# Cosine and sine tables of a long convolution loaded as ready high and low parts, sine layers on 128 partitions, one filter split and one gate projection later

## Chip, cores and metric

The program runs on one NeuronCore of a Trainium2 chip. The metric is the device time of one execution in microseconds, the median over several runs. A profile of one execution, taken by the hardware profiler, goes with it. TensorE is called PE below, VectorE DVE, ScalarE ACT, GpSimd POOL and SyncE SP.

## What is computed

One layer of an encoder on 512 tokens of width 1024. Its mixer projects the normalised input once (`w_in`) and feeds two branches. Branch B, which the change touches, is a Hyena convolution. Its filter comes from a small network with two sine layers. The second branch, HGRN2, and the PEER layer that follows (most of the program's time) are the same before and after.

```python
hid = jnp.sin(freq1 * (z @ w1 + b1))            # z: 512 x 33, hid: 512 x 64
hid = jnp.sin(freq2 * (hid @ w2 + b2))
filt = (hid @ w3) * jnp.exp(-t[:, None] * jnp.abs(decay_rate)[None, :])
...
hy = centred_short_conv(hy, conv_w, conv_b)
x0, x1, v = jnp.split(hy, 3, axis=-1)
y_b = x0 * bidirectional_fftconv(v * x1, h_f, h_b, hyena_bias)
y_b = jnp.einsum('blc,cd->bld', y_b, w_branch_b)
g_a, g_b = jnp.split(gates, N_BRANCHES, axis=-1)
merged = jax.nn.sigmoid(g_a) * y_a + jax.nn.sigmoid(g_b) * y_b
```

## The kernel before

Every float32 product is made of three faster products: each operand is split into a high part (a cast by ACT, L93) and a low part (a subtraction by DVE, L94), and `mm3` (L98 to 105) issues high x high (L102), high x low (L103), and low x high or its mirror (L105). A projection of the 512 tokens onto 128 columns is 24 matmuls of 128x512 into a PSUM tile `ps_mm`, of which there are three buffers. Its weights arrive as `wraw` (512 KB, an SP DMA, L129) and become `whi` (ACT) and `wlo` (DVE), two buffers each.

`hyena` treats the 1024 channels in four quarters (`half` = 0 to 3) of 256. A quarter does, for each of its two blocks of 128 channels, three projections with a short convolution (`conv`: ACT scales the PSUM tile into SBUF at L375, DVE adds the neighbours at L376 and L377, and only L377 frees the PSUM tile), the product x1 * v (L542), sums and differences `sd` of mirrored halves (L546 to 550), transposes on PE (L553, L565), and the splits `uo` and `ue`. After them stand the spectrum of the filter (`spectrum(kept, ...)`), the spectrum of the signal multiplied by it (L612 to 614), the next quarter's filter (`filtered`), and the way back (L628 to 651). The transforms are matmuls with tables of cosines and sines (`co`, `so`, `ee`, `ceT`, `soT`, `coT`, `seT`).

- `setup` (L384) loads seven tables of 256 or 258 KB by SP, splits each with a cast on ACT and a subtraction on DVE, loads the alternating row `alt`, and runs the two sine layers on 64 partitions of 512 elements: a matmul (L429, L432), eight DVE steps (L418 to 424), a Sin on ACT (L425).
- `filtered` (L470) loads `fw3` (ACT's queue in the first quarter, L476), casts it (L480), loads the decay twice (`decb`, L486), takes its absolute value (L487) and the windows `win` (L491), multiplies and folds.
- `parted` (L521) splits the folded filter into f1 and f0; in quarters 1 to 3 it stands ahead of the quarter's loop.
- `gates_b` (L260) is a generator: each `next(fill)` is one projection for the branch's gate (columns 72 + db of `w_in`) that gives PE work while DVE is behind. Seven calls stand in the four quarters (one in the middle of quarters 0, 1 and 2, one behind the spectrum of each). Their results go to DRAM (`gbd`) and come back behind the convolution for the sigmoid (L284). The eighth gate is made there and its sigmoid is read straight from PSUM (L267). Then `yh` and `yl` are split from the convolution's result, and the eight projections with `w_b` follow.

The framework's scheduler puts the instructions of each engine in one order; each engine then runs its list strictly in that order, waiting where an input or a buffer is not ready.

Of the kernel before, what the change touches and what calls it, by code (L numbers as in the profile page):

```python
# [215 lines left out]
def mixer(C):  # L216
# [60 lines left out]
    with tc.tile_pool(name="gb", bufs=1) as cp:  # L277
        yh = cp.tile([P, KB, L], F32R, name="yh")
        yl = cp.tile([P, KB, L], F32R, name="yl")
        for db in (KB - 1, *range(KB - 1)):  # L280
            gts[db] = cp.tile([P, L], F32, name=f"gt{db}")
            if db < KB - 1:
                nc.sync.dma_start(gts[db], C.gbd[db])
                nc.scalar.activation(gts[db], gts[db], AF.Sigmoid)  # L284
# [61 lines left out]
def hyena(C, ctx, xh, xl, raws, fill):  # L346
# [37 lines left out]
    def setup():  # L384

        wide = w2.tile([P, 2, 4, HC], F32, name="dftraw", tag="pm", bufs=1).rearrange("p q t c -> p q (t c)")

# [10 lines left out]
        raw = held(7)
        nc.vector.memset(raw[:, : H + 2], 0.0)
        for row in (0, LOW):  # L400
            nc.sync.dma_start(raw[row : row + 1, : H + 2], a["alt"])
        nc.sync.dma_start(raw[:, H + 2 : H + 3], a["altc"])
        nc.scalar.copy(alt, raw[:, : H + 2])
# [2 lines left out]
        layers = cp.tile([P, 2, L], F32, name="layers", tag="f1h")
        scratch = cp.tile([P, 2, L], F32, name="scratch", tag="f1l")
        zT = layers[:33, 0]
        nc.sync.dma_start(zT, a["zT"])
        fw1 = cp.tile([33, FH], F32, name="fw1")  # L410
        nc.sync.dma_start(fw1, a["f_w1"])
        fw2 = cp.tile([FH, FH], F32, name="fw2")
# [14 lines left out]
        hid1 = layers[:FH, 1]  # L427
        ps = C.ps_x.tile([P, L], F32, name="ps_x")
        nc.tensor.matmul(ps[:FH], fw1, zT, start=True, stop=True)  # L429
        sine_layer(hid1, ps[:FH], "f_b1", "f_q1")  # L430
        ps = C.ps_x.tile([P, L], F32, name="ps_x")
        nc.tensor.matmul(ps[:FH], fw2, hid1, start=True, stop=True)  # L432
        hid = layers[:FH, 0]
        sine_layer(hid, ps[:FH], "f_b2", "f_q2")
        nc.scalar.copy(hid2[:FH], hid)
        nc.vector.tensor_sub(hid2[FH:], hid, hid2[:FH])
# [91 lines left out]
    for half in range(D // HC):  # L528
# [974 lines left out]

def constants():
# [3 lines left out]
    def trig(f, k, t):  # L1508
# [38 lines left out]
def layout(inputs):  # L1547
# [67 lines left out]
```

## Time and profile before

| | |
|---|---|
| median of 3 runs (lowest, highest) | 2027.45 us (2026.8, 2028.96) |
| the profiled execution | 2028.04 us, its span 2026.3 us |
| mean granted clock of PE | 0.994 of full speed |
| busy time of DVE, ACT, POOL | 1665.9 us (82%), 993.2 us (49%), 550.3 us (27%) |
| the convolution's part of the span | about 19 to 291 us |

The profile lists busy time by engine, the waits of an engine with what ended them, and the rows of a timeline: start in us, duration in us, engine, line, output and input, and in brackets the idle time ahead of the row with its releaser. Starts of consecutive rows on one engine are nearer together than the durations say, since work is pipelined. A window row gives, for a stretch of time, each engine's busy time, PE's granted clock (PEclk), the busy share of the DMA engines and GB/s.

### The profile page before, as it was taken

The numbers are of one execution on the slowest core, as the hardware profiler recorded it, in microseconds if no ns is written. First come the engines' busy times: TensorE is split into PE (matmuls) and PEld (weight loads), VectorE is DVE, ScalarE is ACT, GpSimd is POOL, SyncE is SP. The second block draws the span as 40 slices with busy tenths as digits, with TensorE's granted clock in tenths as the row PEclk, the third lists the DMA queues.
The fourth block names the chain that finished last, engine by engine and source line by source line (L and its number), as shares of the span: only waits on it lengthen the run. The fifth ranks groups of instructions, "written<-read, shape, count | busy, mean of one in ns | idle before, by whom it ended". The sixth has DMA issues, their size and how long they took to land.

```text
span 2026.3 us, 32320 instructions
## 1 busy us (share of the span) xinstructions
PE 1993.7 (98%) x12417; PEld 1759.9 (87%) x12417; DVE 1665.9 (82%) x2978; ACT 993.2 (49%) x1466; POOL 550.3 (27%) x331
## 2 busy tenths in 40 slices
PE   8979999999999999999999999999999999999998
PEld 6868878888887898889999998888888888888887
DVE  7888863788988647979999968887897889888895
ACT  6545453777775623436767743333333333333333
POOL 0000000000000000000000027777767767666760
PEclk9989999999999999999999999999999999999999
DMA  5212223222212434214767898988988998898884
GB/s 196 99 48 84 73 94 106 84 82 75 73 67 72 146 136 146 99 68 157 227 203 234 276 336 330 333 335 311 362 315 333 339 361 327 337 346 328 327 299 165
DMA packets 161711, 421.99 MB, mean 208 GB/s; under 512 B 13166, under 2 KB 64628, under 8 KB 161430
## 3 DMA queue, kind: packets, MB, share of 16 engines
q1 hardware_dynamic: 118212, 269.09, 37.7%
q0 software_dynamic: 36864, 134.23, 18.0%
q10 hardware_dynamic: 6482, 16.61, 2.3%
q8 instruction: 97, 1.59, 0.3%
q14 instruction: 56, 0.46, 0.1%
HBM read 380.04 MB, written 39.85 MB: 207 GB/s over the span
## 4 chain that ended last, share of the span: by engine, by line
PE 93%; DVE 4%; ACT 1%; issue 1%; DMA 1%; ACTq 0%; DVEq 0%; SPq 0%
PE ps_mm L102 10%; PE ps_mm L105 10%; PE ps_mm L103 10%; PE acc L1195 9%; PE acc L1194 9%; PE acc L1193 9%; PE ps_a L102 9%; PE ps_a L103 8%; PE ps_a L105 8%; PE ps_g L1480 4%; PE ps_x L751 1%; PE ps_s L1325 1%; PE ps_x L102 1%; PE ps_x L105 1%; PE ps_x L103 1%
## 5 line engine op out<-in xcount | busy, mean ns | idle before, releaser
L94 POOL TENSOR_TENSOR ul<-uraw,uh 128x1024 fp32r<-128x1024 f32 x70 | 186.5, 2665 | 588.2 <-DMA gt<-Gd 434.3
L102 PE MATMUL ps_a<-pxh,uh 128*128 128x384 f32 x1024 | 345.8, 338 | 0.3 <-ACT gact L1045 0.3
L103 PE MATMUL ps_a<-pxl,uh 128*128 128x384 f32 x1024 | 342.3, 334 | 0.0
L1195 PE MATMUL acc<-vh,gl 128*128 128x512 f32 x768 | 300.8, 392 | 0.0
L1194 PE MATMUL acc<-vl,gh 128*128 128x512 f32 x768 | 300.0, 391 | 0.0
L1193 PE MATMUL acc<-vh,gh 128*128 128x512 f32 x768 | 299.2, 390 | 0.0
L102 PE MATMUL ps_mm<-xh,whi 128*128 128x512 f32 (+1 forms) x656 | 258.0, 395 | 10.4 <-DVE x L377 10.4
L93 ACT CAST vh<-vraw 128x1024 fp32r<-128x1024 f32 x128 | 134.6, 1052 | 256.9 <-PE acc L1195 127.2
L103 PE MATMUL ps_mm<-xl,whi 128*128 128x512 f32 (+1 forms) x656 | 256.0, 392 | 0.0
L1136 DVE SCALAR_TENSOR_TENSOR grow<-grow,xg 128x1024 f32<-128x1024 f32 x128 | 193.9, 1534 | 50.4 <-DMA grow<-in_u,gidx 50.2
L1148 DVE SCALAR_TENSOR_TENSOR xg<-grow,gw,xg 128x1024 f32<-128x1024 f32 x127 | 195.9, 1542 | 33.7 <-DMA grow<-in_v,gidx 31.9
L1016 POOL IOTA iota<- 128x512 bf16 x1 | 1.2, 1190 | 762.0 <-PE ps_mm L105 762.0
L1107 POOL DMA_INDIRECT grow<-in_u,gidx x128 | 192.5, 1504 | 36.9 <-issue 24.5
L105 PE MATMUL ps_a<-pxh,ul 128*128 128x384 f32 x1024 | 198.4, 334 | 0.0
L103 PEld LDWEIGHTS ps_a<-pxl,uh 128*128 128x128 f32 x1024 | 192.4, 188 | 3.7
L102 PEld LDWEIGHTS ps_a<-pxh,uh 128*128 128x128 f32 x1024 | 192.3, 188 | 3.7 <-ACT gact L1045 0.6
L93 ACT CAST uh<-uraw 128x1024 fp32r<-128x1024 f32 x128 | 134.7, 1052 | 118.3 <-PE ps_a L103 84.5
L94 DVE TENSOR_TENSOR vl<-vraw,vh 128x1024 fp32r<-128x1024 f32 x128 | 186.9, 1461 | 2.5 <-ACT vh L93 2.5
L94 DVE TENSOR_TENSOR wlo<-wraw,whi 128x1024 fp32r<-128x1024 f32 x112 | 136.5, 1219 | 61.4 <-ACT whi L93 29.0
L1107 POOL DMA_INDIRECT grow<-in_v,gidx x128 | 169.9, 1327 | 35.9 <-issue 21.9
L105 PEld LDWEIGHTS ps_a<-pxh,ul 128*128 128x128 f32 x1024 | 179.3, 188 | 0.0
L93 ACT CAST whi<-wraw 128x1024 fp32r<-128x1024 f32 x112 | 117.5, 1049 | 120.1 <-PE ps_mm L103 115.1
(428 smaller groups left out, 3958.0 us busy)
## 6 DMA issues: line engine op xcount, KB each, us to landing
uraw<-in_uT SPq DMA_DIRECT2D x128, 512.0 KB, 6.4
vraw<-in_v SPq DMA_DIRECT2D x128, 512.0 KB, 5.5
wraw<-in_w_in SPq DMA_DIRECT2D x80, 512.0 KB, 3.3
Gd<-Gs SPq DMA_DIRECT2D x12, 2048.0 KB, 9.9
gt<-Gd SPq DMA_DIRECT2D x32, 768.0 KB, 7.4
kept<-gact ACTq DMA_DIRECT2D x22, 384.0 KB, 3.2
gkept<-kept SPq DMA_DIRECT2D x22, 384.0 KB, 6.0
wraw<-in_w_q SPq DMA_DIRECT2D x16, 512.0 KB, 3.2
```

Source lines behind the costliest of these rows:

```text
L93: nc.scalar.copy(hi, src)
L94: return (eng or nc.vector).tensor_sub(lo, src, hi).ins
L102: nc.tensor.matmul(out, ah, bh, start=(i == 0), stop=False)
L103: nc.tensor.matmul(out, *((al, bh) if late else (ah, bl)), start=False, stop=False)
L105: nc.tensor.matmul(out, *((ah, bl) if late else (al, bh)), start=False, stop=(stop and i == n - 1))
L1107: nc.gpsimd.indirect_dma_start(out=t, out_offset=None, in_=tab, in_offset=bass.IndirectOffsetOnAxis(ap=gidx[:, j : j + 1], axis=0))
L1136: nc.vector.scalar_tensor_tensor(t, t, 1.0, xg, op0=ALU.mult, op1=ALU.mult, accum_out=gdot[h][:, i : i + 1])
L1148: nc.vector.scalar_tensor_tensor(gacc, t, gw[h][:, i : i + 1], gacc, op0=ALU.mult, op1=ALU.add)
L1193: nc.tensor.matmul(acc[k][c], gh[:, ts_], vh[:, ds_], start=(r == 0), stop=False)
L1194: nc.tensor.matmul(acc[k][c], gh[:, ts_], vl[:, ds_], start=False, stop=False)
L1195: nc.tensor.matmul(acc[k][c], gl[:, ts_], vh[:, ds_], start=False, stop=(r == NK - 1))
L1480: nc.tensor.matmul(pg[:, q * P : q * P + P], own[:, q], rows[:, q], start=True, stop=True)
```

## The change

Four edits, all in the convolution:

1. The host supplies the tables already split, in two tensors: `tablesco` (128 x 3072 floats, 1.57 MB: co, so, ee) and `tablesceT` (128 x 4128, 2.11 MB: ceT, soT, coT, seT). Each is loaded by one DMA on POOL's queue into a tile of the split type, held back by a one-element ACT copy out of the last of `xh`. The seven casts, seven subtractions and seven SP DMAs go; `alt` becomes one DMA of 128 x 259.
2. The sine layers work on 128 partitions of 256 elements: `fw1` and `fw2` are block-diagonal 128 x 128, `zT` is 128 x 256.
3. `parted` of quarter 1 stands behind the quarter's loop.
4. The `next(fill)` in the middle of quarter 2 goes. Six gates are made in the convolution, and two (db 6 and 7) behind it.

```diff
-        for db in (KB - 1, *range(KB - 1)):
+        for db in (KB - 2, KB - 1, *range(KB - 2)):
             gts[db] = cp.tile([P, L], F32, name=f"gt{db}")
-            if db < KB - 1:
+            if db < KB - 2:
                 nc.sync.dma_start(gts[db], C.gbd[db])
                 nc.scalar.activation(gts[db], gts[db], AF.Sigmoid)
             else:
-                run(fill)
+                next(fill)
...
-            nc.sync.dma_start(raw, a[name])
-            split(nc, hi, lo, raw)
-            dft[name] = (hi, lo)
...
+        zT = layers[:, 0]
+        nc.sync.dma_start(zT, a["zT"])
...
+        for group, w in ((("co", "so", "ee"), H), (("ceT", "soT", "coT", "seT"), H + 2)):
+            t = cp.tile([P, len(group), 2, 2, w], F32R, name="tables" + group[0])
+            nc.scalar.copy(t[:, 0, 0, 0, 0:1], xh[:, KB - 1, L - 1 :])
+            nc.gpsimd.dma_start(t, a["tables" + group[0]])
+            for i, name in enumerate(group):
+                dft[name] = t[:, i, 0], t[:, i, 1]
+        raw = scratch[:, :, :].rearrange("p a b -> p (a b)")
+        nc.sync.dma_start(raw[:, : H + 3], a["alt"])
         nc.scalar.copy(alt, raw[:, : H + 2])
         nc.scalar.copy(altc, raw[:, H + 2 : H + 3])
...
-        if half:
+        if half > 1:
             fe, fo = parted(*folded)
...
+        if half == 1:
+            fe, fo = parted(*folded)
...
-        if half < D // HC - 1:
+        if half < 2:
             next(fill)
```

ACT near the start, right behind the casts of `xh` (`fw` is the raw of `fw3`, `whi` the high part of the next projection's weights, `x_333` and `vv` the short convolutions of the first block). Before:

```order
L476 DMA fw_612<-in_f_w 64x2x256 x2
L93 CAST soh<-dftraw 128x512
L93 CAST eeh<-dftraw 128x512
L486 DMA decb<-in_f_decay 128x256
L93 CAST whi<-wraw 128x1024
L375 ACTIVATE x_333<-ps_mm,vec 128x512
L480 CAST fw3h<-fw_612 128x512
L93 CAST coTh<-dftraw 128x512
L93 CAST whi<-wraw 128x1024
L375 ACTIVATE vv<-ps_mm,vec 128x512
```

and after:

```order
L469 DMA fw_577<-in_f_w 64x2x256
L479 DMA decb<-in_f_decay 128x256 x2
L473 CAST fw3h<-fw_577 128x512
L93 CAST whi<-wraw 128x1024
L375 ACTIVATE x_333<-ps_mm,vec 128x512
L402 CAST alt<-scratch 128x258
L403 CAST altc<-scratch 128x1
L480 ACTIVATE decb<-decb 128x512
L93 CAST whi<-wraw 128x1024
L484 ACTIVATE win<-decb,vec 128x512
L375 ACTIVATE vv<-ps_mm,vec 128x512
```

The cast of `fw3` now stands ahead of the third projection's `whi`, and `alt`, `decb` and a window stand ahead of the fourth's `whi` and of `vv`. On PE the first block's transposes stand behind 19 matmuls of the third projection, before behind 28 (all 24 of it and 4 of the fourth).

DVE in quarter 1 ahead of the point where a PSUM tile comes free for PE (L377 of `x_1014` before, of `x_979` after: the tile x0 of quarter 1 in both; `x_1115` is x1 of its second block, `vv` that block's v). Before:

```order
L516 TENSOR_TENSOR pm<-once 128x2x256
L94 TENSOR_TENSOR f1l<-pm,f1h 128x1024
L368 TENSOR_TENSOR um<-ps_x,um 1x128
L94 TENSOR_TENSOR f0l<-pm,f0h 128x1024
L376 SCALAR_TENSOR_TENSOR x_1014<-ps_mm,vec,x_1014 128x511
L376 SCALAR_TENSOR_TENSOR vv<-ps_mm,vec,vv 128x511
L377 SCALAR_TENSOR_TENSOR x_1014<-ps_mm,vec,x_1014 128x511
```

and after:

```order
L509 TENSOR_TENSOR pm<-once 128x2x256
L368 TENSOR_TENSOR um<-ps_x,um 1x128
L376 SCALAR_TENSOR_TENSOR x_979<-ps_mm,vec,x_979 128x511
L376 SCALAR_TENSOR_TENSOR x_1115<-ps_mm,vec,x_1115 128x511
L377 SCALAR_TENSOR_TENSOR x_979<-ps_mm,vec,x_979 128x511
L377 SCALAR_TENSOR_TENSOR x_1115<-ps_mm,vec,x_1115 128x511
L376 SCALAR_TENSOR_TENSOR vv<-ps_mm,vec,vv 128x511
L94 TENSOR_TENSOR wlo<-wraw,whi 128x1024
L377 SCALAR_TENSOR_TENSOR vv<-ps_mm,vec,vv 128x511
L94 TENSOR_TENSOR f1l<-pm,f1h 128x1024
```

The splits f1l and f0l have moved behind the release. On PE, 17 projection matmuls stood between the transposes ahead of that wait and the wait; now there are 4, and 48 instead of 24 stand between the wait and quarter 1's filter spectrum. Eleven fewer stand ahead of quarter 0's filter spectrum.

ACT behind the convolution (`gt` the gates, `yh` the high part of the convolution's result, `whi` that of `w_b`). Before:

```order
L93 CAST yh<-yb 128x512 x5
L284 ACT_TABLE_LOAD
L284 ACTIVATE gt_2787<-gt_2787 128x512
L267 ACTIVATE gt_2760<-ps_mm 128x512
L284 ACTIVATE gt_2790<-gt_2790 128x512
L284 ACTIVATE gt_2793<-gt_2793 128x512
L284 ACTIVATE gt_2796<-gt_2796 128x512
L284 ACTIVATE gt_2799<-gt_2799 128x512
L284 ACTIVATE gt_2802<-gt_2802 128x512
L284 ACTIVATE gt_2805<-gt_2805 128x512
L93 CAST yh<-yb 128x512 x3
L93 CAST whi<-wraw 128x1024 x9
```

and after:

```order
L93 CAST yh<-yb 128x512 x5
L284 ACT_TABLE_LOAD
L284 ACTIVATE gt_2751<-gt_2751 128x512
L267 ACTIVATE gt_2691<-ps_mm 128x512
L284 ACTIVATE gt_2754<-gt_2754 128x512
L284 ACTIVATE gt_2757<-gt_2757 128x512
L284 ACTIVATE gt_2760<-gt_2760 128x512
L284 ACTIVATE gt_2763<-gt_2763 128x512
L284 ACTIVATE gt_2766<-gt_2766 128x512
L93 CAST yh<-yb 128x512 x3
L267 ACTIVATE gt_2724<-ps_mm 128x512
L93 CAST whi<-wraw 128x1024 x10
```

One sigmoid of a gate from DRAM has gone, one of a gate in PSUM has come, behind `yh`. The first `w_b` weights, cast during the convolution before, are now the first of the ten `whi` behind that sigmoid.

More of the change, by code (lines that the diff above doesn't have):

```diff
@@ L398, in setup @@
[L398 to L402, printed above, removed]
+        layers = cp.tile([P, 2, H], F32, name="layers", tag="f1h")
+        scratch = cp.tile([P, 2, H], F32, name="scratch", tag="f1l")
+        zT = layers[:, 0]
+        nc.sync.dma_start(zT, a["zT"])
+        fw1 = cp.tile([P, P], F32, name="fw1")
+        nc.sync.dma_start(fw1, a["f_w1"])
@@ new lines, in setup @@
+        fw2 = cp.tile([P, P], F32, name="fw2")
+        nc.sync.dma_start(fw2, a["f_w2"])
+        for group, w in ((("co", "so", "ee"), H), (("ceT", "soT", "coT", "seT"), H + 2)):
[5 more added lines that the diff above has]
+        raw = scratch[:, :, :].rearrange("p a b -> p (a b)")
@@ L403, in setup @@
+        nc.sync.dma_start(raw[:, : H + 3], a["alt"])
         nc.scalar.copy(alt, raw[:, : H + 2])
         nc.scalar.copy(altc, raw[:, H + 2 : H + 3])
[L406 to L412, printed above, removed]
@@ L425, in sine_layer @@
             nc.scalar.activation(dst, arg, AF.Sin)
[L427 to L436, printed above, removed]
+        hid1 = layers[:, 1]
+        ps = psum()
+        nc.tensor.matmul(ps, fw1, zT, start=True, stop=True)
+        sine_layer(hid1, ps, "f_b1", "f_q1")
+        ps = psum()
+        nc.tensor.matmul(ps, fw2, hid1, start=True, stop=True)
+        hid = layers[:, 0]
+        sine_layer(hid, ps, "f_b2", "f_q2")
+        for i in range(2):
+            own, other = slice(i * FH, i * FH + FH), slice((1 - i) * FH, (1 - i) * FH + FH)
+            ns = slice(i * H, i * H + H)
+            nc.scalar.copy(hid2[own, ns], hid[own])
+            nc.vector.tensor_sub(hid2[other, ns], hid[own], hid2[own, ns])
     def odd(dst, mat, fb, src):
@@ L1501, in top16, with short @@
     nc.vector.max_index(idx[:, 8:16], val[:, 8:16], rest)
+def short(t):
+    b = np.ascontiguousarray(t, np.float32).view(np.uint32)
+    return ((b + np.uint32(0x7FF) + ((b >> np.uint32(12)) & np.uint32(1))) & np.uint32(0xFFFFF000)).view(np.float32)
 def constants():
@@ L1525, in constants @@
          "soT": blk(np.concatenate([trig(np.sin, 2 * n + 1, n).T, sign, zero], 1)),
-         "alt": np.concatenate([sign[:, 0], [1.0, 0.0]])[None].astype(np.float32),
-         "altc": sign[:P].astype(np.float32), "ident": np.eye(P, dtype=np.float32)}
+         "ident": np.eye(P, dtype=np.float32)}
+    for group, w in ((("co", "so", "ee"), H), (("ceT", "soT", "coT", "seT"), H + 2)):
+        out = np.zeros((P, len(group), 2, 2, w), np.float32)
+        for i, name in enumerate(group):
+            t = c.pop(name)
+            hi = short(t)
+            out[:, i, 0, :, : t.shape[2]] = hi
+            out[:, i, 1, :, : t.shape[2]] = short(t - hi)
+        c["tables" + group[0]] = out
+    c["alt"] = np.zeros((P, H + 3), np.float32)
+    c["alt"][[0, 32], : H + 2] = np.concatenate([sign[:, 0], [1.0, 0.0]])
+    c["alt"][:, H + 2 :] = sign[:P]
     s = np.arange(P)[:, None] % HALF
@@ L1540, in constants @@
     order = rows(q, H, back, H + P, np.arange(L - 1, H + P, -1), P, np.arange(H + 1, H + P))
-    c["zT"] = np.ascontiguousarray(z[order].T)
+    c["zT"] = np.zeros((P, H), np.float32)
+    for i in range(2):
+        c["zT"][i * (P // 2) : i * (P // 2) + z.shape[1]] = z[order[i * H : i * H + H]].T
     c["pair"] = np.array([PAIR_ID], np.float32)
@@ L1567, in layout @@
     out["v"] = ca(A["peer_v"][0])
-    out["f_w1"] = ca(A["filt_w1"][0])
-    out["f_w2"] = ca(A["filt_w2"][0])
+    for name, w in (("f_w1", A["filt_w1"][0]), ("f_w2", A["filt_w2"][0])):
+        out[name] = np.zeros((P, P), np.float32)
+        for o in (0, P // 2):
+            out[name][o : o + w.shape[0], o : o + w.shape[1]] = w
     out["f_w3"] = ca(A["filt_w3"][0])
@@ L1579, in put @@
         if v.shape[0] == 64:
-            vec[:64, o] = v
+            vec[:64, o] = vec[64:, o] = v
         else:
```

16 lines of the change are left out of this document (4 added, 12 removed).

## Prediction

> **What bounds the kernel now.** I read the page's busy times first, then PE's list of waits (in all, times, longest, in us).
>
> ```profile
> PE 1993.7 (98%) x12417; PEld 1759.9 (87%) x12417; DVE 1665.9 (82%) x2978; ACT 993.2 (49%) x1466; POOL 550.3 (27%) x331
> ```
>
> ```profile
> PE ps_mm L102 <- DVE x L377: 10.4, 1, 10.4
> ...
> PE ps_mm L102 <- ACT yh L93: 3.3, 1, 3.3
> PE ps_x L804 <- ACT vh L715: 1.7, 1, 1.7
> ```
>
> PE is busy for 98% of the span, so a transfer, a cast or a subtraction taken off another engine is worth nothing unless PE waited for it. The convolution holds two waits that are worth anything: 10.4 us in quarter 1, behind DVE's convolution step that frees a PSUM tile, and 3.3 us behind the convolution, for `yh`. Each costs more than its length, as the windows of one microsecond show (the last three numbers are PEclk, the DMA share and GB/s).
>
> ```profile
> 122.00:123.00 1.00, 0.00 (x0) 0.00 (x0) 1.00 (x3) 0.88 (x4) 0.00 (x0) 0.77 0.00 0
> ...
> 136.00:137.00 1.00, 1.00 (x5) 0.77 (x5) 0.94 (x3) 0.74 (x3) 0.00 (x0) 0.91 0.93 336
> ...
> 289.00:290.00 1.00, 0.00 (x0) 0.00 (x0) 0.00 (x0) 1.00 (x3) 0.00 (x0) 0.89 0.00 0
> ...
> 636.00:637.00 1.00, 0.47 (x4) 0.47 (x5) 1.00 (x3) 0.68 (x2) 0.00 (x0) 1.00 0.32 102
> ```
>
> ```profile
> 130.63 0.77 PE L102 MATMUL ps_mm<-xh,whi 128*128 128x512 f32 x1 [10.38 <-DVE x L377]
> ...
> 139.37 0.28 PE L102 MATMUL ps_x<-f1h,coh 128*128 128x256 f32 x1
> ```
>
> The clock granted is 1.00 or 0.50, so a mean of 0.77 means that it fell 2.3 us into the long wait (which began at 130.63 - 10.38 = 120.25), and 0.91 that it rose at 136.18. From 130.63 to there PE ran at half speed: 5.55 us for 2.8 us of work, so 2.8 us lost. At 289 it fell likewise, 2.0 us into the 3.3-us wait (whose end, 291.04, is quoted below). Behind the 1.7-us wait at L804 it stayed at 1.00. A wait of up to 1.7 us therefore costs itself, one of 3.3 us costs itself and 2.8 us, and between them I can't tell.
>
> **The sine layers** save on PE's path. The rows below are the two layers' matmuls.
>
> ```profile
> 53.66 1.07 PE L429 MATMUL ps_x<-layers,fw 33*64 33x512 f32 x2
> ...
> 65.76 1.07 PE L432 MATMUL ps_x<-layers,fw 64*64 64x512 f32 x2
> ```
>
> They take some 1.0 us each. Half the columns make that 0.5 each, so -1.0 us. The shorter DVE and ACT steps and the table casts and subtractions save only what PE waits for, below.
>
> **The start.** The views: PE, the chain of waits (its DMA row), ACT with its DMA issue, and DVE.
>
> ```profile
> 29.27 0.40 PE L102 MATMUL ps_mm<-xh,whi 128*128 128x512 f32 x1
> ...
> 36.67 0.33 PE L553 MATMUL ps_x<-ident,sd 128*128 128x128 f32 x1 [0.86 <-DVE sd L546]
> ```
>
> ```profile
> 22.21 6.64 DMA fw<-in_f_w
> ```
>
> ```profile
> 26.56 1.04 ACT L93 CAST whi<-wraw 128x1024 fp32r<-128x1024 f32 x1
> ...
> 28.93 0.62 ACT L480 CAST fw3h<-fw 128x512 fp32r<-128x512 f32 x1 [0.64 <-DMA fw<-in_f_w]
> ...
> 31.02 0.77 ACT L375 ACTIVATE vv<-ps_mm,vec 128x512 f32<-128x512 f32 x1
> 31.35 0.34 ACTq L486 DMA_DIRECT2D decb<-in_f_decay  x1
> ...
> 32.73 0.41 ACT L403 CAST alt<-dftraw 128x258 fp32r<-128x258 f32 x1
> ...
> 35.13 0.63 ACT L487 ACTIVATE decb<-decb 128x512 f32<-128x512 f32 x1 [0.94 <-DMA decb<-in_f_decay]
> 35.79 0.72 ACT L491 ACTIVATE win<-decb,vec 128x512 f32<-128x512 f32 x1
> ```
>
> ```profile
> 35.12 0.69 DVE L542 TENSOR_TENSOR x<-vv,x 128x512 f32<-128x512 f32 x1
> 35.72 0.69 DVE L481 TENSOR_TENSOR fw3l<-fw,fw3h 128x512 fp32r<-128x512 f32 x1
> 36.32 0.29 DVE L546 TENSOR_TENSOR sd<-x 128x129 f32<-128x129 f32 x1
> ```
>
> ```profile
> 25.00:30.00 5.00, 5.00 (x41) 4.87 (x41) 3.40 (x5) 3.32 (x5) 0.00 (x0) 1.00 0.93 306
> ```
>
> Here the change adds a wait. `whi` of the third projection now queues on ACT behind `fw3h`, and `alt`, `decb` and a `win` queue ahead of the next `whi` and of `vv`, whose product feeds the transposes PE stands before. These small loads share the DMA engines, 93% busy at 306 GB/s already, with 3.7 MB of tables. No row shows a plain DMA on POOL's queue or a DMA that fills a split type, so I bound the landing times. `fw` still lands at 28.85 if the tables only take the place of the seven table loads that ran beside it; earlier if they start late. `decb` is now issued at about 23.7 (an estimate from 22.21: two short copies and two more issues of 0.3 to 0.6); it took 3.8 us in the rows (31.35 to 35.1), and `fw` 6.6 us in the busiest stretch, which gives 27.5 to 30.3. The worst is that it lands last: 3.7 MB of tables and 1.4 MB of other loads at 306 GB/s from 22.2 on is 38.9.
>
> I take `fw` at 28.85 and `decb` no later than 31.6. Then fw3h ends at 29.5, `whi` takes 1.04 and PE starts the third projection at 30.6, not 29.27: 1.3 us. ACT goes on with x (ends 31.2), alt and altc (31.6), decb (32.2), whi (33.2), win (33.8) and vv (34.6). DVE adds two convolution steps (0.66 each), the product (0.60 from 35.12 to 35.72) and sd (0.29): 36.75. PE reaches the transposes 19 matmuls in, at 30.6 + 19 x 0.228 = 34.9, and waits 1.85 us. Both waits are near 1.7, so full clock. Against the 0.86 us of before: **+2.3 us**. From 31.6 on every microsecond of `decb` counts, and the clock falls besides: `decb` at 38.9 gives +12.5. If both land in time (`fw` by 26, `decb` by 28.6), vv ends at 31.6, sd at 33.8 against PE's 33.6: -0.6.
>
> **The wait in quarter 1.** Between quarter 0's product and the release DVE is without a gap but one of 0.59 us.
>
> ```profile
> 98.85 0.69 DVE L612 TENSOR_TENSOR t<-ps_x,kA 128x512 f32<-128x512 f32 x1 [0.92 <-PE ps_x L105]
> ...
> 119.50 0.42 DVE L368 TENSOR_TENSOR fm<-pm,fm 1x256 fp32r<-1x256 f32 x1 [0.59 <-ACT fm L367]
> ...
> 125.77 1.21 DVE L94 TENSOR_TENSOR f1l<-pm,f1h 128x1024 fp32r<-128x1024 f32 x1
> 126.99 0.28 DVE L368 TENSOR_TENSOR um<-ps_x,um 1x128 fp32r<-1x128 f32 x1
> ...
> 128.43 0.74 DVE L376 SCALAR_TENSOR_TENSOR x<-ps_mm,vec,x 128x511 f32<-128x511 f32 x1
> 129.09 0.74 DVE L376 SCALAR_TENSOR_TENSOR vv<-ps_mm,vec,vv 128x511 f32<-128x511 f32 x1
> 129.75 0.74 DVE L377 SCALAR_TENSOR_TENSOR x<-ps_mm,vec,x 128x511 f32<-128x511 f32 x1
> ```
>
> PE starts that stretch of DVE's (0.92 us of waiting at 98.85), and in the new order it does so 11 matmuls (2.5 us) and the sine layers' 1.0 us earlier: 3.5 us. What stood at 125.77 stands at 122.27. Then um 0.28, two steps of 0.66 and one of 0.74 free the tile at 124.6 instead of 130.5, and PE goes on at 124.75. But of the 17 matmuls that ran ahead of the wait only 4 are left. PE stops at 120.25 - 3.5 - 13 x 0.228 = 113.8 and waits 10.95 us, no less than now. Behind it stand 48 matmuls, not 24: 10.9 us, 2.8 for the clock, 0.5 for transposes (139.37 - 130.63 less 24 matmuls and the 2.8), so quarter 1's filter spectrum starts at 138.95 instead of 139.37. From the start to here that is **-0.4 us** in all, the sine's -1.0 within it. So the split's new place brings the release forward and the order gives it back. If DVE gained none of the 3.5 us it would be +3.1; if the 24 were done ahead of the wait after all, -5.9.
>
> **Quarter 2 and behind the convolution.** A gate is 24 matmuls, 5.48 us (279.87 to 285.35, below). Taking it out of quarter 2 makes PE come 5.5 us sooner to products of DVE; the next row shows the cover.
>
> ```profile
> 208.56 0.69 DVE L612 TENSOR_TENSOR t<-ps_x,kA 128x512 f32<-128x512 f32 x1 [4.94 <-PE ps_x L105]
> ```
>
> DVE sat 4.9 us idle there waiting for PE; without the gate it is just ready, and I charge 0 (0.6 at worst). Quarter 3 has no such gate now, and no wait of it is on PE's list. The gate comes back behind the convolution, where PE's rows and ACT's are:
>
> ```profile
> 279.87 0.40 PE L102 MATMUL ps_mm<-xh,whi 128*128 128x512 f32 x1
> ...
> 285.35 0.39 PE L102 MATMUL ps_mm<-yh,whi 128*128 128x512 f32 x1
> ...
> 291.04 0.80 PE L102 MATMUL ps_mm<-yh,whi 128*128 128x512 f32 x1 [3.26 <-ACT yh L93]
> ```
>
> ```profile
> 282.23 2.71 ACT L93 CAST yh<-yb 128x512 fp32r<-128x512 f32 x5 [0.76 <-DVE yb L651]
> ...
> 287.26 3.21 ACT L284 ACTIVATE gt<-gt 128x512 f32<-128x512 f32 x6
> 290.38 1.65 ACT L93 CAST yh<-yb 128x512 fp32r<-128x512 f32 x3
> ```
>
> Before, this place loses 3.3 + 2.8 = 6.1 us. After, on the same clock of times, the second gate ends at 290.83. ACT has five sigmoids instead of six at 0.52 (ends 289.86), `yh` (1.65, 291.5), the sigmoid of the second gate (0.5, 292.0), and only then `w_b`'s first `whi` (1.04, 293.05), for which PE waits until 293.2: 2.4 us. `yh` is no longer late; that cast is. At half clock afterwards the place loses 5.2: **-0.9 us**; with the clock kept, -3.7. I take the half clock, since both falls came within 2.3 us. [...]
>
> **Sum:** 2.3 - 0.4 - 0.9 = +1.0 on the profiled execution's 2028.04, so **2029.0 us**. That execution was 0.6 above the median of 2027.45; a measurement of this kernel can tell about 0.2%, 4.1 us, from no change.
>
> **Rivals.**
> 1. *The tables hold up the small loads* (slower). It decides once `decb` lands behind 31.6. For it: 3.7 MB against 306 GB/s is 12 us of all engines. Against: round robin could let small loads through. If the DMA engines work the tables off in blocks, a block of eight rows of 12 KB (98 KB at 306/16 GB/s each) holds an engine 5.1 us and one of eight of 16.5 KB 6.9 us, and `decb` comes between the two or behind, at about 36: vv ends at 39.0, sd at 41.2, PE waits 6.3 + 1.3 - 0.86 and loses 2.8 of clock: +9.6 in place of 2.3, so 2036.3. [...]
> 2. *The clock stays up behind the convolution*: 2.8 less, 2026.2. For it: 2.4 us is nearer to 1.7 than to 3.3.
> 3. *The small loads land early and the clock stays up* (faster): -0.6 - 0.4 - 3.7, 2023.3. For it: POOL's queue may start late. Against it: `fw` was late in the rows without the tables' extra bytes.
> 4. *The wait in quarter 1 does shrink*: -5.9 in place of -0.4, 2023.5. Against it stands the order.
>
> **Chances:** forecast 0.28, rival 1 0.28, rival 2 0.17, rival 3 0.17, rival 4 0.10. Rival 1 is slower unless `decb` lands before 33; 3 and 4 lie at the edge of 0.2%. So faster 0.20, same 0.51, slower 0.29. The range leaves out the far ends of 1, 3 and 4: 2022.0 to 2037.0.
>
> **What would show it.** Right: a wait for `sd` of about 2 us at 35 us; a wait of about 11 us for L377 near 114 to 125; one of about 2.4 us for `whi` behind the convolution; none in quarters 2 and 3. Wrong: ACT idle for `decb` or `alt` past 32 us with PE's clock at 0.50 near 40 (rival 1); a wait in quarter 1 under 8 us (rival 4); PE waiting for `tablesco` or `tablesceT`.

## The result, and the profile after

The changed kernel takes 2037.53 us in the median of 5 runs (2036.17 to 2041.99), against 2027.51 before on the same chip: a ratio of 1.0053, 95% interval 1.0038 to 1.0068, so slower. The prediction of 2029.0 us (2022.0 to 2037.0) was wrong. Rival 1, that the tables hold up the small loads, had given 2036.3. The profiled execution took 2040.89 us with a span of 2038.7, 12.4 us more than the span before.

PE's list of waits after the change (in all, times, longest, in us):

```profile
PE ps_x L546 <- DVE sd L539: 13.4, 4, 12.5
PE ps_mm L102 <- DVE x L377: 11.1, 1, 11.1
...
PE ps_mm L102 <- ACT whi L93: 2.4, 1, 2.4
```

The waits in quarter 1 (11.1 us) and behind the convolution (2.4 us for `whi` instead of 3.3 for `yh`) are those forecast. The one for `sd` was 0.9 us at its longest before, was forecast at 1.85, and is 12.5. ACT's timeline around it shows whom everybody waits for:

```profile
22.23 1.09 ACTq L479 DMA_DIRECT2D decb<-in_f_decay  x2
26.30 0.62 ACT L473 CAST fw3h<-fw 128x512 fp32r<-128x512 f32 x1 [4.41 <-DMA fw<-in_f_w]
26.82 1.05 ACT L93 CAST whi<-wraw 128x1024 fp32r<-128x1024 f32 x1
27.78 0.77 ACT L375 ACTIVATE x<-ps_mm,vec 128x512 f32<-128x512 f32 x1
39.87 0.41 ACT L402 CAST alt<-scratch 128x258 fp32r<-128x258 f32 x1 [11.33 <-DMA scratch<-in_alt]
...
40.28 0.62 ACT L480 ACTIVATE decb<-decb 128x512 f32<-128x512 f32 x1
40.81 1.03 ACT L93 CAST whi<-wraw 128x1024 fp32r<-128x1024 f32 x1
...
42.37 0.76 ACT L375 ACTIVATE vv<-ps_mm,vec 128x512 f32<-128x512 f32 x1
```

`fw` is early (26.30), so the third projection loses nothing. Then ACT stands 11.33 us before the cast of `alt`, and the fourth projection's `whi` and the scaling of `vv` stand behind it in ACT's list. `alt` was issued on SP right behind a weight load, with the tables issued on POOL at the same time (first two fences: the issues on SP and on POOL; third: the list of DMAs from 18 to 60 us with their size and the median time from issue to landing):

```profile
22.34 0.61 SPq L129 DMA_DIRECT2D wraw<-in_w_in  x1
22.99 0.43 SPq L401 DMA_DIRECT2D scratch<-in_alt  x1
```

```profile
22.11 0.72 POOL L397 DMA_DIRECT2D tablesco<-in_tablesco  x1 [21.65 <-ACT tablesceT L396]
22.82 0.58 POOL L397 DMA_DIRECT2D tablesceT<-in_tablesceT  x1
```

```profile
q0 software_dynamic: 288, 3.69, 23.0%
...
tablesceT<-in_tablesceT POOLq DMA_DIRECT2D x1, 2064.0 KB, 16.8
tablesco<-in_tablesco POOLq DMA_DIRECT2D x1, 1536.0 KB, 10.7
...
decb<-in_f_decay ACTq DMA_DIRECT2D x2, 128.0 KB, 11.0
```

The tables land at 22.82 + 16.8 = 39.6, and `alt`, of 130 KB, with them. POOL's queue (q0) moved its 3.69 MB in 288 packets, one for each row of 12 or 16 KB and a few more.

On PE the loss is the wait and a stretch at half clock behind it (PEclk is 0.50 from 45 to 50 us and 0.85 from 50 to 51); the rows are the end of the wait, the first sine matmul, and the filter spectra of quarters 1 and 2 (before: 53.66, 139.37, and 202.14 in the next fence):

```profile
45.81 0.48 PE L546 MATMUL ps_x<-ident,sd 128*128 128x128 f32 x1 [12.54 <-DVE sd L539]
...
67.11 0.59 PE L419 MATMUL ps_x<-layers,fw 128*128 128x256 f32 x2
...
151.86 0.28 PE L102 MATMUL ps_x<-f1h,tablesco 128*128 128x256 f32 x1
...
209.72 0.28 PE L102 MATMUL ps_x<-f1h,tablesco 128*128 128x256 f32 x1
...
301.01 0.50 PE L102 MATMUL ps_mm<-yh,whi 128*128 128x512 f32 x1 [2.41 <-ACT whi L93]
...
394.78 1.50 PE L799 MATMUL ps_x<-vh,KT 128*128 128x128 f32 x12
```

```profile
202.14 0.28 PE L102 MATMUL ps_x<-f1h,coh 128*128 128x256 f32 x1
...
385.29 1.50 PE L804 MATMUL ps_x<-vh,KT 128*128 128x128 f32 x12
```

The execution after began its transposes of the input 0.43 us earlier (10.48 against 10.91). From there on, against before:

| stretch | measured | forecast |
|---|---|---|
| to the first sine matmul | +13.9 | +2.3 |
| to quarter 1's filter spectrum (84.75 against 85.71) | -1.0 | -0.4 |
| to quarter 2's (57.86 against 62.77), less a gate of 5.48 | +0.6 | 0 |
| to the first `vh,KT` matmul of HGRN2 (185.06 against 183.15), the gate back | -3.6 | -0.9 |

With the early beginning that is +9.5, nearly the +10.0 of the medians. The profiled execution lost another 2.7 us between 1080 and 1680, in the PEER layer, whose lists of instructions are the same before and after (its row of 1.1 us for `vl`, L1189, is part of it).

### The profile page after: what moved, and what is told of

The parts are those of the page before. It is cut to its first block, busy times and chain, and to the rows that moved or that the text cites. A ratio compares the mean times of both kernels' runs of the same rounds, so it can differ in the third digit from the quotient of the medians.

```text
span 2038.7 us, 32292 instructions
## 1 busy us (share of the span) xinstructions
PE 1992.7 (98%) x12417; PEld 1759.5 (86%) x12417; DVE 1660.7 (81%) x2971; ACT 985.8 (48%) x1461; POOL 550.3 (27%) x333
## 4 chain that ended last, share of the span: by engine, by line
PE 80%; DVE 2%; issue 2%; DMA 1%; ACT 0%; POOL 0%; DVEq 0%; POOLq 0%; ACTq 0%
PE ps_a L102 8%; PE ps_a L103 8%; PE ps_a L105 8%; PE ps_mm L102 8%; PE ps_mm L103 8%; PE ps_mm L105 8%; PE acc L1189 8%; PE acc L1190 8%; PE acc L1188 8%; PE ps_g L1475 4%; PE ps_x L746 1%; PE ps_s L1320 1%; DVE grow L1131 1%; DMA grow<-in_u,gidx 1%; DMA gkept<-kept 1%
## 5 line engine op out<-in xcount | busy, mean ns | idle before, releaser
L1189 PE MATMUL acc<-vl,gh 128*128 128x512 f32 x768 | 300.5, 391 | 1.1 <-DVE vl L94 1.1
L102 PE MATMUL ps_mm<-xh,whi 128*128 128x512 f32 (+1 forms) x656 | 258.1, 395 | 11.1 <-DVE x L377 11.1
L1143 DVE SCALAR_TENSOR_TENSOR xg<-grow,gw,xg 128x1024 f32<-128x1024 f32 x127 | 191.3, 1507 | 25.2 <-DMA grow<-in_v,gidx 23.4
```

What stands on the lines that cost most here:

```text
L102: nc.tensor.matmul(out, ah, bh, start=(i == 0), stop=False)
L1143: nc.vector.scalar_tensor_tensor(gacc, t, gw[h][:, i : i + 1], gacc, op0=ALU.mult, op1=ALU.add)
L1189: nc.tensor.matmul(acc[k][c], gh[:, ts_], vl[:, ds_], start=False, stop=False)
```

## The experiments

In all of them the time is compared with the kernel before on the same chip. A short name stands for each kernel.

### The tables back (tables_back)

```diff
-            nc.gpsimd.dma_start(t, a["tables" + group[0]])
+            nc.sync.dma_start(raw, a[name])
+            split(nc, hi, lo, raw)
```

> The changed kernel with its first edit undone: the seven tables are loaded raw by SP and split by ACT and DVE as before; the sine layers on 128 partitions, the later split in quarter 1, the missing gate in quarter 2 and the one-piece load of `alt` stay. Theory (the tables' DMA holds up `alt`): the two traces put the loss before the first sine matmul, 13.9 us there (53.66 - 10.91 = 42.75 us from the first transpose before, 67.11 - 10.48 = 56.63 after), and a gain behind it: -1.0 up to quarter 1's filter spectrum, +0.6 in quarter 2, -3.6 behind the convolution. So this kernel should take 2027.5 - 4.0 = 2023.5 us, with no wait for `sd` over 1.5 us. Rival A (the loss comes from one of the other edits, the order of ACT's list among them): it stays near 2037. Rival B (the four edits only gain together): about 2027.5.

2026.07 us, ratio 0.9992 (0.9983 to 1.0001). The wait for `sd` is 1.7 us at its longest:

```profile
PE ps_mm L102 <- DVE x L377: 11.2, 1, 11.2
...
PE ps_x L552 <- DVE sd L545: 2.2, 2, 1.7
```

So the loss is the first edit's, and rival A is out. The other three together gain 4.1 us in this trace up to HGRN2, as expected, but 1.9 in the median, and the interval reaches no change.

### Shorter rows: 1, 4 and 8 KB (small_rows, rows4k, rows8k)

```diff
-            t = cp.tile([P, len(group), 2, 2, w], F32R, name="tables" + group[0])
+            t = cp.tile([P, len(group), 2, 2, w + 2], F32R, name="tables" + group[0])[:, :, :, :, :w]
```

That is small_rows; rows4k leaves the two spare floats once a table, rows8k once for two tables (three DMAs, the `ceT` group first).

> The changed kernel with one difference: each table row of 256 or 258 floats gets two more floats of room in the SBUF tile, so that the same 3.7 MB on the same queue at the same time go in pieces of 1 KB instead of 12 and 16 KB. The order of every engine is that of the changed kernel. Theory with shared bandwidth (the tables were issued first and take the DMA engines' time, whatever their pieces): `alt` lands with the tables again, near 40, and the time stays at 2037 (2034 to 2040). Theory with long pieces (the DMA engines take a piece from each queue in turn, and `alt` stands behind the pieces of four other SP loads, each of which lets a table row of 12 or 16 KB by): with 1 KB pieces `alt` lands by 30 and the wait for `sd` falls below 3 us: 2024 to 2028.

> The changed kernel with the tables' rows in pieces of 4 KB (one piece a table), between the 1 KB of small_rows and the 12 and 16 KB of the changed kernel; all else stays. Theory (DMA engines take pieces from the queues in turn, so that a queue's share goes with the length of its pieces): `alt` lands between small_rows' 31.3 and the changed kernel's 39.9, near 35, the time lies between 2029.75 and 2037.4, near 2033. Rival (one threshold: short enough pieces all act alike): as small_rows, 2029 to 2030. Rival B (only the number of bytes counts, and small_rows was better because POOL's queue fills more slowly with 3616 pieces): near 2037.

> The changed kernel with its table rows in pieces of 8 KB: `ceT` with `soT` and `coT` with `seT` as one piece each (8.25 KB), `co` with `so` as one of 8 KB, `ee` one of 4 KB, the `ceT` group first, one DMA more on POOL's queue; all else stays. It stands between 4 KB (`alt` lands at 31.7, hardly later than the 30.3 without any table in flight) and 12 to 16 KB (39.9). Theory (each DMA engine takes pieces from its queues in turn; about 16 pieces of SP's queue, its share of the weights and of `alt`, stand ahead when the tables start, so that 16 table pieces go by): 16 x 8.25 KB at the 22 GB/s of one engine are 6 us: `alt` lands at 35 to 37, the time is 2033 to 2035. Rival (up to some length pieces act alike): 31 to 32.5 and 2029 to 2030.5. Rival B (above 4 KB the queue is held until the tables are through): near 39, 2036 or more.

Measured: small_rows 2029.75 us (1.0007; 0.9998 to 1.0016), rows4k 2029.73 (1.0010; 1.0001 to 1.0020), not the 2033 that was expected of it, and rows8k 2032.94 (1.0023; 1.0013 to 1.0032). ACT's cast of `alt`, which starts as soon as `alt` has landed, in small_rows, rows4k and rows8k:

```profile
31.32 0.41 ACT L402 CAST alt<-scratch 128x258 fp32r<-128x258 f32 x1 [3.39 <-DMA scratch<-in_alt]
```

```profile
31.75 0.41 ACT L403 CAST alt<-scratch 128x258 fp32r<-128x258 f32 x1 [3.96 <-DMA scratch<-in_alt]
```

```profile
35.11 0.41 ACT L404 CAST alt<-scratch 128x258 fp32r<-128x258 f32 x1 [6.64 <-DMA scratch<-in_alt]
```

To compare executions that did not begin at the same moment, count from SP's first issue of this stretch, that of `zT` (L389): 20.68, 20.52 and 20.13 in these three, 20.89 in the changed kernel and 20.76 in tables_late (below), where no table is in flight and `alt` is cast at 30.32. The same bytes, issued on the same queue at the same point, then delay `alt` by 1.1 us in pieces of 1 KB, 1.7 at 4 KB, 5.4 at 8 KB and 9.4 at 12 and 16 KB. An estimate of the turns: SP's queue has 16 pieces an engine in the weights and `alt` if they are spread evenly (two times 128 rows over 16 engines), and 16 pieces of the tables at 22 GB/s an engine (353 GB/s of the changed kernel's window from 25 to 30 us, over 16 engines) are 0.7, 3.0, 6.0 and 10.4 us. So the theory of turns, each of which lets a piece of the tables by, came out for rows8k, which was told ahead; for rows4k it had asked for more than was found, and the time there was the rival's. That pieces of up to 8 KB act alike is out, and so is a pure share by bytes (rival B); that pieces of up to 4 KB act nearly alike is not.

The trace's records of the single pieces show the turns themselves. From 27 to 36 us in the changed kernel POOL's queue began 203 pieces, SP's 198 and ACT's 203 (those of 4 bytes left out). The pieces of `alt` begin in rounds there, the first ones at 31.56, 32.27, 32.97 and 33.68, and in alt_pool (below) in rounds of 16, 0.71 us apart; a piece of 16.5 KB at 22 GB/s is 0.75 us. Shorter pieces went by more than one at a turn: from 27 to 30 us 192 on POOL's queue against 139 and 112 at 4 KB, 688 against 145 and 135 at 1 KB. One thing beside the length differs: the tables' first piece begins 3.1 us after the issue of `zT` in the changed kernel, but 5.4, 5.5 and 5.8 us after it at 8, 4 and 1 KB. So part of the step from 8 KB to 12 and 16 KB is the earlier beginning; why it is earlier stays open.

### The tables later (after_small, tables_late)

```diff
-            nc.scalar.copy(t[:, 0, 0, 0, 0:1], xh[:, KB - 1, L - 1 :])
+            nc.gpsimd.tensor_copy(t[:, 0, 0, 0, 0:1], x0[:, n, 0:1])
```

(tables_late, with n = 0 for `tablesco` and 1 for `tablesceT`; after_small copies from `alt` and from `decb`.)

> The changed kernel with the tables held back until the small loads have landed: POOL copies one element out of `alt` (after its cast) and out of `decb` ahead of each table's DMA; everything else stays. Theory (the tables hold up `alt` and `decb`): both land by 28, ACT casts `alt` right behind the short convolution at 28.6 instead of 39.87, the wait for `sd` is below 2 us, and the 13.9 us of the start go: 2023.5, up to 3 more if the tables, now at 29 to 41, hold up the weights of the sixth projection (2023 to 2027). Rival A (`alt` is late because it stands behind the weights on SP's queue): it lands near 40 as before: 2037. Rival B (the order of ACT's and PE's lists costs the time, with `alt` on time): a wait of 6 us or more for `sd` remains: 2030 or more.

> The changed kernel with the tables held back further: POOL copies the first element of `tablesco` out of the first block's x0 and that of `tablesceT` out of the second block's, so that the two loads start near 47 and 60 us, apart from each other. Theory: no load of the start is disturbed, and each table load (5 and 7 us of all DMA engines) fits beside the weights' loads: 2023.5 (2022.5 to 2025), about the same as with the tables behind the small loads or up to 3 us better. If the weights' loads are what the tables disturb, a wait for `whi` appears near 50 to 70 us and the time is 2026 or more. Rival A (the start's loss is not the tables' DMA): 2037.

2028.52 us (1.0003; 0.9994 to 1.0012) and 2028.37 (1.0001; 0.9992 to 1.0010): 9 us of the changed kernel's 10 come back, but not the 13.9 that both were to bring. What is left is at the same place. PE's waits and ACT's list in tables_late, and its first transposes and first sine matmul on PE:

```profile
PE ps_x L546 <- DVE sd L539: 4.3, 3, 3.5
```

```profile
30.32 0.41 ACT L402 CAST alt<-scratch 128x258 fp32r<-128x258 f32 x1 [3.34 <-DMA scratch<-in_alt]
...
32.02 1.04 ACT L93 CAST whi<-wraw 128x1024 fp32r<-128x1024 f32 x1
32.96 0.77 ACT L375 ACTIVATE vv<-ps_mm,vec 128x512 f32<-128x512 f32 x1
```

```profile
10.44 1.11 PE L206 MATMUL ps_x<-ident,xn 128*128 128x128 f32 x4 [0.28 <-DVE xn L249]
...
57.23 0.59 PE L419 MATMUL ps_x<-layers,fw 128*128 128x256 f32 x2
```

With no table in flight `alt` still lands 7.4 us after its issue, behind a weight load of 512 KB on the same queue, and 1.7 us of short steps follow. PE waits 3.5 us and then runs at half clock for a while (PEclk is 0.50 from 38 to 39 us and 0.60 from 39 to 40). So rivals A and B of after_small each had a part of it.

### `alt` away from ACT, and the order on ACT (alt_pool, order_only, small_late)

```diff
-        nc.scalar.copy(alt, raw[:, : H + 2])
+        nc.gpsimd.tensor_copy(alt, raw[:, : H + 2])
...
```

```diff
+        with tc.issue_after(C.first_block):
+            nc.scalar.copy(alt, raw[:, : H + 2])
...
+            with tc.issue_after(C.first_block):
+                nc.scalar.activation(decb, decb, AF.Abs)
```

The first is alt_pool (`altc` goes to POOL too). The second is order_only (on the changed kernel) and small_late (on tables_late): `C.first_block` is ACT's step L375 for the first block's `vv`, and the casts of `altc` and `fw3` move behind it as well.

> The changed kernel with one difference: the casts of `alt` and `altc` are made by POOL, which is idle there, instead of ACT; the tables are loaded as in the changed kernel. So ACT no longer waits for `alt`, but still for `decb`. Theory (the tables hold up both, `alt` to 39.8 and `decb` to about 33.9, from its issue at 22.8 and the 11.0 us of its landing): the absolute value of `decb` starts near 34 instead of 40.28, PE waits 6 to 7 us for `sd` instead of 12.5, and the time is about 2031. Rival A (`decb` too lands with the tables, near 39): 2036 or more. Rival B (`decb` had landed by 28, only `alt` was late): a wait under 3 us, 2027 or less.

> The changed kernel with its tables loaded at the start as they are, and only ACT's list changed: the casts of `alt`, `altc` and `fw3` and the absolute value of `decb` stand behind the first block's `vv`. Theory (the tables' load costs only through what stands behind it on ACT's list): ACT waits for `alt` until 39.8 all the same, but the third and fourth projections' weights and `vv` are out by then; what then is late is the fifth projection's `whi` (needed near 38.7, out near 44 behind alt, `fw3h`, decb and two windows): a wait of 3 to 5 us with some half clock: 2027 to 2031. Rival A (nothing else is late): 2023.3, as small_late. Rival B (the weights' loads on SP suffer too, so that PE waits for the fourth projection's `whi` already): 2033 or more.

> The kernel with the tables held back until the blocks' x0 (tables_late), and in it the casts of `alt`, `altc` and `fw3` and the absolute value of `decb` stand on ACT behind the first block's `vv` instead of ahead of it. tables_late still lost 4.0 us before the first sine matmul, with no table in flight: ACT waited 3.3 us for `alt`, and four short steps stood ahead of the `whi` and `vv` that the transposes need. Theory (that order is the rest of the start's loss): `vv` is scaled by 30 and PE waits under 1 us for `sd`; first sine matmul within 0.6 us of before's; 3.5 to 4 us less than tables_late's 2028.37, so 2024.5. Rival (the rest lies in the place of the transposes on PE, 8 matmuls earlier than before, or in the weights' loads): a wait of 2 us or more remains, 2027 or more.

alt_pool: 2037.33 us (1.0047; 1.0033 to 1.0060), no better. Taking `alt` off ACT's list uncovers `decb`, which lands with the tables as well (rival A; my 33.9 was wrong):

```profile
38.72 0.63 ACT L480 ACTIVATE decb<-decb 128x512 f32<-128x512 f32 x1 [10.45 <-DMA decb<-in_f_decay]
```

order_only: 2033.44 us (1.0031; 1.0021 to 1.0042). The time is rival B's, the cause another: `whi` and `vv` are out by 28.9, but the cast of `fw3` now stands behind `alt` on ACT, and on DVE the low part of `fw3` (`fw3l`, L475) stands ahead of the last step of `vv`, the product and `sd`. So DVE waits 8.4 us for ACT and PE 8.3 for `sd`. I had expected 3 to 5, behind the fifth `whi`, and overlooked DVE's list. ACT, DVE and PE:

```profile
28.13 0.78 ACT L375 ACTIVATE vv<-ps_mm,vec 128x512 f32<-128x512 f32 x1
37.45 0.41 ACT L403 CAST alt<-scratch 128x258 fp32r<-128x258 f32 x1 [8.54 <-DMA scratch<-in_alt]
...
37.86 0.61 ACT L474 CAST fw3h<-fw 128x512 fp32r<-128x512 f32 x1
```

```profile
38.51 0.69 DVE L475 TENSOR_TENSOR fw3l<-fw,fw3h 128x512 fp32r<-128x512 f32 x1 [8.37 <-ACT fw3h L474]
```

```profile
40.97 0.47 PE L550 MATMUL ps_x<-ident,sd 128*128 128x128 f32 x1 [8.32 <-DVE sd L543]
```

small_late: 2023.26 us (0.9977; 0.9968 to 0.9986), the first kernel faster than before. No wait for `sd` of more than 0.7 us is left, and the first sine matmul comes 0.7 us sooner after the first transposes than before. So the start's 13.9 us have two parts: 9.8 are the tables loaded so early (the changed kernel against tables_late, 56.6 and 46.8 us from the first transpose to the first sine matmul), 8.0 of them their long rows (48.6 us in small_rows); and the rest, with 0.7 that before had lost too, is the list of ACT. The two rows of small_late, 42.1 us apart:

```profile
10.48 1.12 PE L206 MATMUL ps_x<-ident,xn 128*128 128x128 f32 x4 [0.27 <-DVE xn L249]
...
52.56 0.59 PE L420 MATMUL ps_x<-layers,fw 128*128 128x256 f32 x2
```

### The other edits one by one (sine_only, tb_split, tb_gate)

sine_only is the kernel before with the second edit alone. tb_split and tb_gate are tables_back with the third or the fourth edit undone:

```diff
-        if half > 1:
+        if half:
             fe, fo = parted(*folded)
...
```

```diff
-        if half < 2:
+        if half < D // HC - 1:
             next(fill)
...
```

> The kernel before with the second edit alone: the sine layers on 128 partitions; tables, `parted` and gates as before. The prediction's term: -1.0 us. Theory now: PE's list moves with it (in the kernel with old tables and the early split quarter 0's filter spectrum came 3.4 us earlier from the first sine matmul on), but PE then stands before the same DVE stretch in quarter 1, and its wait grows from 10.4 to about 13 us: -1.0 to +0.5, not to be told from no change (2027 to 2028.5), and the trace shows quarter 1's filter spectrum no more than 1 us earlier than before. Rival (the move is worth its 3.4 us): 2025 or less.

> The kernel with the tables loaded the old way (tables_back) and in it the third edit undone as well: `parted` of quarter 1 stands ahead of the quarter's loop again. Theory (the later split brings the release forward and the order on PE gives it back): from the first sine matmul to quarter 1's filter spectrum tables_back took 1.27 us less than before, 1.0 of it the sine layers'; so undoing the split costs about 0.3 us, 2026.4 against 2026.07. Rival (the wait for L377 shrinks by the later split): 2 us or more are lost, 2028 or more, and the wait is longer than tables_back's 11.2 us. Rival 2 (the later split itself costs, since only 4 matmuls run ahead of the wait): 2 to 3 us are gained, 2024 or less.

> The kernel with the tables loaded the old way (tables_back) and in it the fourth edit undone as well: seven gates in the convolution again, one behind it. Theory: in tables_back's trace the edit takes 4.6 us off quarter 2 and gives 1.9 back behind the convolution, where a 2.4-us wait for `whi` keeps PE's clock at 1.00 instead of the 3.3-us wait for `yh` with 2.8 us of half clock: 2.7 us in that execution. In executions where the clock falls in the 2.4-us wait too, the edit is worth about nothing. So undone it should cost 1 to 2.7 us: 2027 to 2028.8, with the 3.3-us wait back. Rival (the edit is worth nothing or costs, as the wait for `whi` replaces the one for `yh`): 2026 or less.

sine_only: 2031.07 us, ratio 1.0019 (1.0010 to 1.0028): slower, where the prediction had -1.0 us and the expectation no change. tb_split: 2028.03 (0.9996; 0.9987 to 1.0005), tb_gate: 2028.58 (1.0002; 0.9993 to 1.0011), against tables_back's 0.9992. The row that ends the wait in quarter 1, in sine_only, in tb_split and in tables_back, with the filter spectrum of quarter 1 behind it:

```profile
127.16 0.76 PE L102 MATMUL ps_mm<-xh,whi 128*128 128x512 f32 x1 [13.25 <-DVE x L377]
...
140.78 0.28 PE L102 MATMUL ps_x<-f1h,coh 128*128 128x256 f32 x1
```

```profile
127.99 0.76 PE L102 MATMUL ps_mm<-xh,whi 128*128 128x512 f32 x1 [13.35 <-DVE x L377]
...
141.54 0.28 PE L102 MATMUL ps_x<-f1h,coh 128*128 128x256 f32 x1
```

```profile
125.55 0.77 PE L102 MATMUL ps_mm<-xh,whi 128*128 128x512 f32 x1 [11.19 <-DVE x L377]
...
138.71 0.28 PE L102 MATMUL ps_x<-f1h,coh 128*128 128x256 f32 x1
```

Before, the release stood at 130.63 with 10.38 us of waiting and 24 matmuls between it and the spectrum. In sine_only it comes 3.5 us sooner, but 48 projection matmuls stand behind it, and the spectrum comes 1.4 us later (140.78 against 139.37; the start of the two is the same within 0.1 us). So it is the sine layers' edit that moves 24 matmuls behind the wait (11 from ahead of quarter 0's filter spectrum, 13 from between it and the wait), not the split's new place: tb_split, with the split in its old place, has the same 48. Put later, the split brings the release 2.1 us forward (127.99 against 125.55, less the executions' starts of 11.30 and 10.96) and the spectrum 2.5: the rival of tb_split was right. In the medians tb_split and tables_back are 0.0004 apart, less than their intervals. The gate's removal brings 4.5 us in the traces up to HGRN2 and 0.0010 in the ratios, 2 us, as expected, though here too the two intervals overlap.

### Faster kernels (both_late, no_sine)

```diff
+        raw = fetch_w(C, a["w_b"][0])
...
+        with tc.issue_after(cast):
+            cast = nc.scalar.copy(now[0], raw).ins
...
+        with tc.issue_after(cast):
+            for db in range(KB - 2):
+                nc.scalar.activation(gts[db], gts[db], AF.Sigmoid)
```

both_late adds this to small_late (the first `cast` is the last cast of `yh`); no_sine is both_late with the sine layers on 64 partitions, as before the change.

> The kernel with late tables and late small steps (small_late), and behind the convolution ACT's list in another order: all eight casts `yh`, then the cast of `w_b`'s first weights, and only then the six sigmoids of the gates from DRAM. small_late still waits 2.5 us there for that cast. Theory: `yb` is complete at 282 (in the trace of before), so `yh` and the cast are done by 287, before the second gate's matmuls end; the 2.5-us wait goes, and no half clock can follow it: 2023.26 - 2.5 = 2020.8, with less spread. Rival (the first product of `w_b` then waits for its gate's sigmoid, or `yl` on DVE is late): a wait of 1 us or more takes its place, 2022 to 2023.5.

> The fastest kernel so far (both_late, 2020.89) with the second edit undone: the sine layers on 64 partitions of 512 elements again. Alone on the kernel before, the second edit cost 3.7 us in the median (1.8 in the trace up to the end of the convolution), since it brought PE 11 matmuls sooner to the DVE stretch of quarter 1 and left 11 more behind the wait. Theory (with the split later the release comes 2 us sooner and that order no longer costs): undoing it costs the layers' own 1.0 us or nothing: 2021 to 2022. Rival (the second edit costs here too): 2019.5 or less.

both_late: 2020.89 us (0.9963; 0.9949 to 0.9976), as expected; no wait for `whi` or `yh` is left behind the convolution. no_sine: 2017.88 us (0.9953; 0.9939 to 0.9966), so the rival was right: the sine layers' edit costs here too, 4.2 us in the traces up to HGRN2; the two intervals of the ratios overlap. The release and the spectrum in no_sine, then in both_late:

```profile
126.40 0.77 PE L102 MATMUL ps_mm<-xh,whi 128*128 128x512 f32 x1 [7.96 <-DVE x L385]
...
132.27 0.28 PE L102 MATMUL ps_x<-f1h,tablesco 128*128 128x256 f32 x1
```

```profile
123.50 0.77 PE L102 MATMUL ps_mm<-xh,whi 128*128 128x512 f32 x1 [10.94 <-DVE x L385]
...
137.42 0.28 PE L102 MATMUL ps_x<-f1h,tablesco 128*128 128x256 f32 x1
```

With the sine layers on 64 partitions PE has more projection matmuls ahead of its wait, waits 3 us less, and has 16 of them left behind it instead of 48.

## Why the prediction was wrong

**The start** is the step that failed: "I take `fw` at 28.85 and `decb` no later than 31.6." `fw` landed by 26.3, earlier than that. `decb` landed near 38.7 (seen in alt_pool), and `alt`, for whose landing the step had no estimate at all, at 39.9: it stood behind 512 KB of weights on SP's queue and behind the tables. The term of +2.3 measured +13.9. The mechanism was near that of rival 1, DMA engines that work the tables off in long pieces, and the prediction's own upper bound of +12.5 (all bytes first, 38.9) was nearly it. But rival 1 had blocks of eight rows, which no run shows, and counted on `decb` alone; the traces show turns of one row (203 pieces of the tables to 198 of SP's queue in 9 us), and `alt` as late as `decb`. So that its 2036.3 came so near to 2037.5 is in part luck. The round robin, which the prediction held against rival 1, is what delayed `alt`: each of its turns let a row of 12 or 16 KB by (rounds of 0.71 us in alt_pool). The runs with shorter rows show the mechanism, and the late tables the size, 9.8 us. The 1.3 us taken for `whi` of the third projection did not come about. The order on ACT alone, for which the 2.3 us stood, cost 4.7 (46.8 against 42.1 us, tables_late and small_late), since `alt` landed late even so (cast at 30.32 in tables_late) and the wait of 3.5 us brought half clock with it.

**The sine layers**, -1.0 us on PE: the layers' matmuls did get shorter (0.59 for 1.07), but the edit moves PE's list, and alone it costs (1.0019; 3.7 us in the median, of which the trace shows 1.8 up to HGRN2). What the step saves on PE is lost when PE then waits for DVE (13.25 us in sine_only, 10.38 before), and I had said that only of DVE's and ACT's steps.

**The wait in quarter 1** came out at 11.07 us against 10.95, and its sum at -1.0 against -0.4. Its working saw both movements but not which edit makes which: "the split's new place brings the release forward and the order gives it back." The order is the sine layers' doing; the split alone gains some 2 us in the traces. So the near agreement is in part two edits that cancel.

**Quarter 2** cost the 0.6 us named as the worst. **Behind the convolution** the wait of 2.41 us for `whi` was forecast at 2.4, but the clock stayed at 1.00 (window row in the last section): -3.6, near rival 2's -3.7, instead of -0.9. Rival 2's reason, that 2.4 us is nearer to 1.7 than to 3.3, was not what decided; the place of the wait on the clock's grid did (last section).

**What stays open.** The runs of one kernel lie 2 to 8 us apart, those of before 2 to 6. Part of it is the PEER layer, in which the profiled executions of the changed kernel and of sine_only lost 2.7 and 3.5 us, the changed kernel with the same lists of instructions as before. Why was not tried.

## What to carry to other kernels

A bulk load in long rows is not free because nobody waits for it: ask which small loads are issued beside it and what stands behind them on an engine that works in order; issue it after them, or cut its rows (here 2037.53 us became 2028.37 with the late tables and 2029.73 with rows of 4 KB). Before a wait on the slowest engine's stretch, count the matmuls ahead of it and behind it: an edit that brings PE there sooner moves work to the wrong side of the wait. A measured neighbour on each side of a disputed price (here 1, 4, 8 and 16 KB; waits of 1.7 and 3.3 us) says more than either bound.

## What the runs showed of the hardware

In the profiled executions PE's granted clock changed at points of a grid of 3.41 us. In the changed kernel it falls at 36.64 and at 132.22 (from the shares in the windows below), 95.58 us or 28 times 3.413 apart; before at 122.54 and 289.78, 49 times. In rows8k it changes at 34.70, 44.94, 126.88 and 137.12 (3, 24 and 3 times), in tables_late at 36.38, 39.80 and 121.72 (1 and 24), in sine_only at 117.84 and 131.52 (4), in no_sine at 122.90 and 129.74 (2). Of the interval that ended at such a point PE had been idle 2.01 and 2.29 us before, 1.94 in alt_pool and 1.78 in tb_gate, and the clock fell; 1.80 in tables_late, 1.74 in tb_gate and 1.69 at HGRN2's wait, and it stayed. So less than the whole interval was enough; what decides near 1.8 us was not shown. The 2.41-us wait behind the convolution was cut by a grid point (299.5) into 0.87 and 1.54 us, and the clock stayed, as it did in the profiled executions of all eleven kernels with a wait of 2.0 to 2.8 us there. In each of them a grid point cut the wait, and none of the parts was longer than the 1.80 us in tables_late. That was no accident: in all eleven that point was the 46th, 157.0 us, after the clock's last rise, so the place went with the rise behind quarter 1's wait. One of 2.65 us at the start of after_small lay in one interval (2.57 us of it) and lost the clock. So in these runs a wait of 2.0 to 2.8 us cost the clock or not by where it lay on the grid. Windows of the changed kernel (third to last number: PEclk):

```profile
36.00:37.00 1.00, 0.00 (x0) 0.00 (x0) 0.00 (x0) 0.00 (x0) 0.00 (x0) 0.82 0.95 314
...
132.00:133.00 1.00, 0.00 (x0) 0.00 (x0) 1.00 (x3) 0.00 (x1) 0.00 (x0) 0.61 0.00 0
...
299.00:300.00 1.00, 0.00 (x0) 0.00 (x0) 1.00 (x3) 1.00 (x4) 0.00 (x0) 1.00 0.00 0
```
